# Attention stage of a hybrid layer: one group of small matmuls per block instead of two

## The chip, the cores and the metric

The kernel runs on one core of a Trainium2 chip. The metric is device microseconds of one execution. An execution that was profiled has a time of its own, and its trace spans nearly all of that time. The engines are TensorE (PE, its weight loads apart as PEld), VectorE (DVE), ScalarE (ACT), GpSimd (POOL) and SyncE (SP), each with a program of its own that it works through in order; semaphores tie them together.

## The reference, cut to what matters

One layer: an input projection, then dilated window attention beside an RWKV-7 recurrence, an output projection, and a mixture of experts. The change concerns the attention. It has 12 heads of width 64 in three groups with windows and dilations (128, 1), (512, 4) and (2048, 16); within a group each block of 128 queries sees its own 128 keys and, where there is one, the block before.

```python
p = h @ w_in
q, k, v, p_rwkv, p_gate = jnp.split(p, [...], axis=-1)
q = rms_norm(heads(q), q_norm_gain[:, None, :])
k = rms_norm(heads(k), k_norm_gain[:, None, :])
...
# per group: blocks of W queries against 2 W keys
s = jnp.einsum('bdhnqe,bdhnke->bdhnqk', qb, kb).astype(jnp.float32) * (E ** -0.5) + bias
s = jnp.where(valid, s, NEG_INF)
lse = jax.nn.logsumexp(s, axis=-1)
p = jnp.exp(s - lse[..., None])
o = jnp.einsum('bdhnqk,bdhnke->bdhnqe', p.astype(v.dtype), vb)
...
# the three groups are weighted by softmax over their lse, then projected
wts = jax.nn.softmax(jnp.stack(lses, axis=0), axis=0)
att = jnp.einsum('gbsh,gbshe->bshe', wts, jnp.stack(outs, axis=0))
mixed = gates[..., :D] * y_att + gates[..., D:] * y_rwkv
```

The sequence is 1024 long, the model 1024 wide.

## The kernel before

**Stages.** After a first stage (norm, the input projection's RWKV part, the recurrence) comes the attention stage, here from about 548 us on; at its end the output projections follow (from L1089), then the mixture of experts, which loads the weights of 32 experts. The scheduler that orders instructions by itself has been closed before the attention stage: there every engine runs in the order in which the code is written.

**Fillers.** The input projection is made of matmuls with 128x512 operands (L306, `pa<-...`, called F here), three per product, because each 32-bit factor is split in two halves. They are not run by themselves: they stand in generators in the list `fillers`, and `fill(n)` issues the next n of them. So the 1007 F of the attention stage lie between its small matmuls: 144 to a unit (the q, k and v of the next one) and, in the last unit, the columns of the gates (`rest`). An F of the gates ends, each 24, in an evacuation: VectorE L381, ScalarE L382, a store.

**Units and blocks.** There are six units (three groups, two pairs of heads), each of eight blocks. The loop at L1044 to L1070 does for each block: `fill(FA)`, 9 F; `ptrans` (L984), the transposes of the probabilities (L989, called T) and their copy to SBUF by ScalarE (L991); `scores` of the next block (L969, matmuls L976, called S; bias by VectorE L977, row maximum L979, exponentials by ScalarE L981); `fill(FU)`, 9 F; `values` (L993, matmuls L1002, called V), whose sums ScalarE copies to `Og` each fourth block (L1009). With two blocks of keys T and V are four products, with one they are two; the trace counts V, S and the two-column matmuls below twice, as two passes each.

**What else stands in the loop.** In block 1 `finish` closes the unit before: transposes of the row maxima and sums (L1019), copies by ScalarE, stores of `Og` (L1027) and `dML` (L1029) on SyncE's queue. For the last unit `finish` stands behind the loop; the later weights stand behind its stores on SyncE's queue, and `MLc`, which is loaded back from `dML` (L1109), is what the weighting of the groups begins with. In blocks 3, 4 and 5 one step each of the `prelude` of the next unit is made. Its second step are the sums of squares of q and k: 16 matmuls with two columns (L940), with two F behind every second one; VectorE makes inverse roots of them (L251 and on), GpSimd spreads those (L950), and the third step transposes these (L958) and makes the keys.

Of the kernel before, what the change touches and what calls it, by code (L numbers as in the profile page):

```python
# [23 lines left out]
NH = 8  # L24
C = 64
DEC = math.exp(-0.5)
FT, FS, FP, FA, FU, GL = 20, 6, 2, 9, 9, 10
FI, FQ, TP, FR, SQ, SG, SB, UJ, QW, QL, QT, QJ = 14, 2, 1, 16, 1, 0, 1, 1, 1, 0, 0, 1
LP, LB, LR, PF, MP, QB, GB, NY = 0, 0, 0, 1, 0, 1, 2, 2
DILS = (1, 4, 16)  # L30
# [151 lines left out]
def block_kernel(ctx, tc, I, out, dbg=None):  # L182
# [36 lines left out]
    def cc(name, i=None):  # L219
        lo, hi = CV[name]  # L220
        return cv[:, lo:hi] if i is None else cv[:, lo + i:lo + i + 1]
# [58 lines left out]
    def pb(shape):  # L280
        return psB.tile([128] + shape, F32, name="pb")
# [73 lines left out]
    for h in range(2):  # L355
        pt = psB.tile([128, 4, 128], F32, name="pb")
        for j in range(4):
            i = 4 * h + j
# [6 lines left out]
    def tstep(n=1):  # L365
        for _ in range(n):
            if side and next(side[0], 1) == 1:
                side.pop(0)
# [21 lines left out]
    def fill(n):  # L390
        while n > 0 and fillers:
            try:
                next(fillers[0])
                n -= 1
                filled[0] += 1
                if filled[0] % FI == 0:
                    tstep()
            except StopIteration:
                fillers.pop(0)
# [3 lines left out]
    def need(key):  # L403
        while key not in done:
            fill(1)
# [476 lines left out]
    def perm(ap, dil, h=None):  # L882
        L = S // dil
        v = ap.rearrange("q (r l) -> q l r", r=dil)
        return v if h is None else v[:, h * L // 2:(h + 1) * L // 2, :]
# [28 lines left out]
    def prelude(u):  # L914
        g, hp = u.g, u.hp
        nat = lambda ap: ap.rearrange("q (l r) -> q l r", r=u.dil)
        u.qT, kr, vT = qkv.pop((g, hp))
        u.bias = p4.tile([128, 2, 256], F32, name="bias")
        nb = 128 if g == 2 else 256
        for hh in range(2):  # L920
            nc.sync.dma_start(u.bias[:, hh, 256 - nb:], dBias[g, 2 * hp + hh][:, 256 - nb:])
        if g == 2:
            nc.gpsimd.memset(u.bias[64:128, :, 128:192], NEG)
        sqs = []
        for n, src in enumerate((u.qT, kr)):
            sq = p4.tile([128, S], F32, name="sq")
            nc.scalar.activation(sq, src, AF.Square)
            sqs.append(sq)
        u.Vt = p4.tile([128, 8, 128], F32, name="Vt")
        for h in range(2):  # L930
            pt = pb([4, 128])
            for j in range(4):
                i = 4 * h + j
                nc.tensor.transpose(pt[:, j], vT[:, 128 * i:128 * i + 128], ident)
            nc.scalar.activation(u.Vt[:, 4 * h:4 * h + 4], pt, AF.Copy)
        yield
        pn = pb([2, 8, 2])
        for n in range(2):
            for j in range(8):
                nc.tensor.matmul(pn[:, n, j], sqs[n][:, 128 * j:128 * j + 128], cc("ind2"), start=True, stop=True)  # L940
                if j % 2 == 1:
                    fill(2)
        u.rn = p4.tile([128, 2, 8, 2], F32, name="rqk")
        rsqrt(u.rn.rearrange("q a b c -> q (a b c)"), pn.rearrange("q a b c -> q (a b c)"), (1.0 / 64, 1e-6), None,
              [128, 32])
        nc.vector.tensor_scalar(u.rn[:, 0], u.rn[:, 0], 0.125, None, op0=ALU.mult)
        rnbs = []
        for h in range(2):
            rnb = p4.tile([128, 8, 64], F32, name="rkb")
            nc.gpsimd.tensor_tensor(rnb, u.rn[:, 1, 4 * h:4 * h + 4].rearrange("q a b -> q (a b)")[:, :, None]  # L950
                                    .to_broadcast([128, 8, 64]), one_t[:, :, None].to_broadcast([128, 8, 64]), op=ALU.mult)
            rnbs.append(rnb)
        yield
        u.kT = p4.tile([128, S], F32, name="kT")
        for h in range(2):
            pt = pb([4, 128])
            for j in range(4):
                nc.tensor.transpose(pt[:, j], rnbs[h][:, 2 * j:2 * j + 2, :].rearrange("q a b -> q (a b)"), ident)  # L958
            nc.vector.scalar_tensor_tensor(perm(u.kT, u.dil, h), nat(kr[:, h * 512:(h + 1) * 512]), gqk[:, g:g + 1],
                                           nat(pt.rearrange("q a b -> q (a b)")), op0=ALU.mult, op1=ALU.mult)  # L960
        u.Og = p4.tile([128, S], F32, name="Og")
        u.ML = p4.tile([128, 8, 4], F32, name="ML")
        nc.gpsimd.memset(u.ML[:, :, 2:4], 0.0)

    def keys(u, i):
        prev = (u.g == 0 and i > 0) or (u.g == 1 and i % 2 == 1)
        return (256, 128 * i - 128) if prev else (128, 128 * i)

    def scores(u, i):  # L969
        nk, ko = keys(u, i)  # L970
        Sb = p4.tile([128, 2, 256], F32, name="Sb", bufs=3)
        u.Sb = Sb
        for hh in range(2):
            hr = hrs[hh]
            pS = pb([256])
            nc.tensor.matmul(pS[:, 0:nk], u.qT[hr, 128 * i:128 * i + 128], u.kT[hr, ko:ko + nk], start=True, stop=True)  # L976
            nc.vector.scalar_tensor_tensor(Sb[:, hh, 0:nk], pS[:, 0:nk], u.rn[:, 0, i, hh:hh + 1],  # L977
                                           u.bias[:, hh, 256 - nk:], op0=ALU.mult, op1=ALU.add)
        nc.vector.tensor_reduce(u.ML[:, i, 0:2], Sb[:, :, 0:nk], axis=AX.X, op=ALU.max, negate=True)  # L979
        for hh in range(2):  # L980
            nc.scalar.activation(Sb[:, hh, 0:nk], Sb[:, hh, 0:nk], AF.Exp, bias=u.ML[:, i, hh:hh + 1],  # L981
                                 accum_out=u.ML[:, i, 2 + hh:3 + hh])

    def ptrans(u, i):  # L984
        nkb = keys(u, i)[0] // 128
        pP = pb([2, 2, 128])
        for hh in range(2):
            for kb in range(nkb):
                nc.tensor.transpose(pP[:, hh, kb], u.Sb[:, hh, 128 * kb:128 * kb + 128], ident)  # L989
        u.PT = p4.tile([128, 2, 2, 128], F32, name="PT")  # L990
        nc.scalar.activation(u.PT[:, :, 0:nkb], pP[:, :, 0:nkb], AF.Copy)  # L991

    def values(u, i):  # L993
        nk, ko = keys(u, i)
        nkb = nk // 128
        dil, L = u.dil, S // u.dil
        if i % 4 == 0:
            u.pO = pb([4, 128])
        for hh in range(2):
            for kb in range(nkb):  # L1000
                b = ko // 128 + kb
                nc.tensor.matmul(u.pO[hrs[hh], i % 4], u.Vt[:, b, 64 * hh:64 * hh + 64], u.PT[:, hh, kb],  # L1002
                                 start=(kb == 0), stop=(kb == nkb - 1))
        if i % 4 == 3:
            po_ = u.pO.rearrange("q a b -> q (a b)")
            if dil > 1:
                r0 = (i // 4) * (512 // L)
                o = u.Og.rearrange("q (l r) -> q r l", r=dil)[:, r0:r0 + 512 // L, :]
                nc.scalar.activation(o, po_.rearrange("q (r l) -> q r l", l=L), AF.Copy)  # L1009
            else:  # L1010
                nc.scalar.activation(u.Og[:, 128 * (i - 3):128 * (i + 1)], po_, AF.Copy)
# [22 lines left out]
    for g in range(3):  # L1034
        for hp in range(2):
            u = Unit()
# [7 lines left out]
    for _ in prelude(units[0]):  # L1044
        fill(24)
    scores(units[0], 0)
    for n, u in enumerate(units):
        nxt = units[n + 1] if n + 1 < len(units) else None
        for i in range(8):
            fill(FA)  # L1050
            ptrans(u, i)
            if i < 7:
                scores(u, i + 1)
            elif nxt is not None:
                scores(nxt, 0)
            if i == 1 and n > 0:
                finish(units[n - 1])
            if nxt is not None:
                if i == 3:
                    need(key(n + 1))  # L1060
                    pre = prelude(nxt)
                    if n + 2 < len(units):
                        fillers.append(qkv_steps(*key(n + 2)))
                    else:
                        fillers += rest
                if 3 <= i < 6:
                    next(pre, None)
            fill(FU)
            values(u, i)
    finish(units[-1])  # L1070
    s3.close()

# [627 lines left out]
```

## Time and profile before

| | us |
|---|---|
| Median of three runs | 1754.18 |
| Lowest and highest | 1747.92, 1766.67 |
| The profiled execution | 1749.15 |
| Its span in the trace | 1747.4 |
| TensorE busy | 1667.3 (95%) |
| VectorE busy | 1204.8 (69%) |
| ScalarE busy | 871.5 (50%) |
| GpSimd busy | 299.8 (17%) |

The shares are means over stages of different kinds. The page's 40 slices, of 44 us each, show the attention stage as the 13th to the 22nd: TensorE at nine tenths or more in all but the last of them, VectorE at three to six tenths, DMA at one tenth for most of it. TensorE's granted clock is a row of tenths of full speed there, and a column (PEclk) in the view by windows: 1.00 is 2.4 GHz, 0.50 is 1.2 GHz. In the view by time a row is one instruction or several of one kind in a row (x8), with its start, its busy time, and in brackets the idle time of its engine before it with what ended that. Matmuls overlap, so busy times of neighbours exceed the distance of their starts; costs are read from starts.

### The profile page before, as it was taken

What the parts mean: (1) busy time and instruction counts of PE and PEld (TensorE: products, weight loads), DVE (VectorE), ACT (ScalarE), POOL (GpSimd) and SP (SyncE); (2) the same over time, 40 slices, a digit from 0 to 9 for tenths busy, and PEclk for the clock granted to TensorE, in tenths of its full rate; (3) what the DMA queues carried; (4) which work ended last, traced back from release to release, by engine and by line L of the source; (5) the groups of instructions that cost most, each with busy time, mean ns of one, the idle gap of its engine ahead of it and who ended that gap; (6) DMA issues with size and microseconds to landing.
All of it is one profiled execution on the core that took longest, in us unless ns stands there. A gap on an engine that the chain in (4) does not pass through costs nothing. (4 is left out here: it accounts for less than half of the span.)

```text
span 1747.4 us, 25870 instructions
## 1 busy us (share of the span) xinstructions
PE 1667.3 (95%) x9395; PEld 1321.3 (76%) x9396; DVE 1204.8 (69%) x2181; ACT 871.5 (50%) x1315; POOL 299.8 (17%) x321
## 2 busy tenths in 40 slices
PE   8999999999999999999998899979999999999996
PEld 6677777777777777777777677758888888888884
DVE  5647798575664444344436666589999999998985
ACT  4523434332231233343344122278888888887774
POOL 0110113123432000000000131112222221221211
PEclk9998999799999999999999899979999999999998
DMA  8323333355762111111138884479999999999993
GB/s 292 138 74 125 95 107 115 110 193 180 232 205 85 37 38 42 43 50 43 52 113 272 253 291 144 182 250 372 375 380 373 371 368 368 371 364 372 360 371 114
DMA packets 145619, 363.44 MB, mean 208 GB/s; under 512 B 17316, under 2 KB 62772, under 8 KB 145484
## 3 DMA queue, kind: packets, MB, share of 16 engines
q1 hardware_dynamic: 123108, 303.67, 48.1%
q0 software_dynamic: 15872, 50.35, 10.3%
q10 hardware_dynamic: 6504, 7.69, 1.6%
q8 instruction: 76, 1.25, 0.3%
q14 instruction: 59, 0.48, 0.1%
HBM read 307.49 MB, written 62.29 MB: 212 GB/s over the span
## 5 line engine op out<-in xcount | busy, mean ns | idle before, releaser
L1529 PE MATMUL pb<-u,xTh 128*128 128x512 f32 x1024 | 338.6, 406 | 0.5 <-ACT xTh L1524 0.5
L306 PE MATMUL pa<-xlo,wh 128*128 128x512 f32 x736 | 307.6, 418 | 0.0
L306 PE MATMUL pa<-xhi,wl 128*128 128x512 f32 x736 | 302.3, 411 | 2.2 <-DVE wl L277 2.2
L306 PE MATMUL pa<-xhi,wh 128*128 128x512 f32 x736 | 301.5, 410 | 1.5 <-DVE raw L426 1.0
L1415 DVE TENSOR_TENSOR u<-raw,u 128x1024 fp32r<-128x1024 f32 x216 | 255.0, 1219 | 18.1 <-ACT u L1414 14.6
L1414 ACT ACTIVATE u<-raw 128x1024 fp32r<-128x1024 f32 x216 | 223.7, 1056 | 31.6 <-PE pb L1529 19.7
L1529 PEld LDWEIGHTS pb<-u,xTh 128*128 128x128 f32 x1024 | 191.4, 189 | 40.5 <-ACT xTh L1524 1.4
L1529 PE MATMUL pb<-u,xTl 128*128 128x512 f32 x512 | 207.7, 406 | 0.3 <-DVE xTl L1525 0.3
L306 PEld LDWEIGHTS pa<-xlo,wh 128*128 128x128 f32 x736 | 141.2, 192 | 40.7 <-issue 11.0
L306 PEld LDWEIGHTS pa<-xhi,wl 128*128 128x128 f32 x736 | 141.6, 192 | 34.4 <-issue 3.3
L306 PEld LDWEIGHTS pa<-xhi,wh 128*128 128x128 f32 x736 | 141.4, 192 | 34.4 <-issue 2.9
L1415 DVE TENSOR_TENSOR u<-mix,u 128x1024 fp32r<-128x1024 f32 x128 | 151.5, 1218 | 11.2 <-ACT u L1414 9.1
L1529 PE MATMUL pa<-u,hTh 128*128 128x512 f32 x512 | 143.4, 401 | 0.9 <-ACT hTh L1524 0.9
L1414 ACT ACTIVATE u<-mix 128x1024 fp32r<-128x1024 f32 x128 | 133.2, 1057 | 16.6 <-PE pb L1529 9.2
L977 DVE SCALAR_TENSOR_TENSOR Sb<-pb,rqk,bias 128x128 f32<-128x128 f32 (+1 forms) x96 | 35.5, 407 | 124.5 <-PE pb L976 116.6
L1508 POOL DMA_INDIRECT out<-row,tba x30 | 78.5, 2617 | 202.5 <-ACT u L1414 171.9
L1529 PEld LDWEIGHTS pb<-u,xTl 128*128 128x128 f32 x512 | 96.9, 189 | 18.5 <-DVE xTl L1525 1.0
L1529 PEld LDWEIGHTS pa<-u,hTh 128*128 128x128 f32 x512 | 93.5, 188 | 22.4 <-ACT hTh L1524 1.5
L275 ACT ACTIVATE wh<-wr 128x1024 fp32r<-128x1024 f32 x49 | 51.8, 1056 | 113.5 <-PE pa L306 95.1
L1529 PE MATMUL pa<-u,hTl 128*128 128x512 f32 x256 | 80.7, 396 | 1.2 <-DVE hTl L1525 1.2
L1502 POOL DMA_INDIRECT xin<-dH,tbl x32 | 38.5, 1203 | 250.7 <-PE pb L1523 247.5
L981 ACT ACTIVATE Sb<-Sb,ML 128x128 f32<-128x128 f32 (+1 forms) x96 | 42.3, 442 | 54.7 <-DVE ML L979 54.7
(415 smaller groups left out, 2872.8 us busy)
## 6 DMA issues: line engine op xcount, KB each, us to landing
raw<-in_w_expert_up SPq DMA_DIRECT2D x72, 512.0 KB, 11.7
raw<-in_w_expert_gate SPq DMA_DIRECT2D x71, 512.0 KB, 4.9
raw<-in_w_expert_down SPq DMA_DIRECT2D x71, 512.0 KB, 11.8
wr<-in_w_in SPq DMA_DIRECT2D x49, 512.0 KB, 3.5
mix<-in_w_expert_down SPq DMA_DIRECT2D x46, 512.0 KB, 13.5
mix<-in_w_expert_gate SPq DMA_DIRECT2D x42, 512.0 KB, 5.0
mix<-in_w_expert_up SPq DMA_DIRECT2D x40, 512.0 KB, 11.8
dGA<-gs POOLq DMA_DIRECT2D x32, 256.0 KB, 3.3
```

What stands on the lines that cost most here:

```text
L275: nc.scalar.activation(wh, wr, AF.Copy)
L306: nc.tensor.matmul(ps, a[:, k, :], b[:, k, hs], start=(n == 0), stop=(n == 23))
L977: nc.vector.scalar_tensor_tensor(Sb[:, hh, 0:nk], pS[:, 0:nk], u.rn[:, 0, i, hh:hh + 1], u.bias[:, hh, 256 - nk:], op0=ALU.mult, op1=ALU.add)
L981: nc.scalar.activation(Sb[:, hh, 0:nk], Sb[:, hh, 0:nk], AF.Exp, bias=u.ML[:, i, hh:hh + 1], accum_out=u.ML[:, i, 2 + hh:3 + hh])
L1414: nc.scalar.activation(hi, raw, AF.Copy)
L1415: nc.vector.tensor_tensor(lo, raw, hi.bitcast(F32), op=ALU.subtract)
L1502: nc.gpsimd.indirect_dma_start(out=dst, out_offset=None, in_=src, in_offset=bass.IndirectOffsetOnAxis(ap=idx, axis=0), bounds_check=S - 1, ...
L1508: nc.gpsimd.indirect_dma_start(out=out, out_offset=bass.IndirectOffsetOnAxis(ap=idx, axis=0), in_=src, in_offset=None, compute_op=ALU.add)
L1529: nc.tensor.matmul(ps, x, w, start=first, stop=last)
```

## The change

The matmuls of a block are put in one group: `values` moves from the end of its block to the front of the next block's group, ahead of its `ptrans`; `fill(FU)` goes, and `fill(FA)` issues 20 F instead of 9. The last block's `values` stands behind the loop, with its own `fill(FA)` ahead. In the prelude the F between the matmuls of L940 go. Lines behind L940 move up by 2 up to the loop, so that V is L1000, T L987, S L974, and the last unit's L1019 is L1017; L1089 becomes L1091.

```diff
-FT, FS, FP, FA, FU, GL = 20, 6, 2, 9, 9, 10
+FT, FS, FP, FA, GL = 20, 6, 2, 20, 10
@@ prelude
                 nc.tensor.matmul(pn[:, n, j], sqs[n][:, 128 * j:128 * j + 128], cc("ind2"), start=True, stop=True)
-                if j % 2 == 1:
-                    fill(2)
@@ the loop over units and blocks
     scores(units[0], 0)
+    last = None
     for n, u in enumerate(units):
         nxt = units[n + 1] if n + 1 < len(units) else None
         for i in range(8):
             fill(FA)
+            if last is not None:
+                values(*last)
+            last = u, i
             ptrans(u, i)
...
                 if 3 <= i < 6:
                     next(pre, None)
-            fill(FU)
-            values(u, i)
+    fill(FA)
+    values(*last)
     finish(units[-1])
```

*One block.* TensorE's program in the second block of the first unit, before: T and S as one group, nine F, V as another (`pa` and `pb` are PSUM tiles, `Sb` the probabilities, `PT` their transposes, `Vt` the values).

```order
L306 MATMUL pa<-xlo,wh 128x512
L989 MATMUL pb<-ident,Sb 128x128 x4
L976 MATMUL pb<-kT,qT 128x256 x2
L306 MATMUL pa<-xhi,wl 128x512
...
L306 MATMUL pa<-xlo,wh 128x512
L1002 MATMUL pb<-PT,Vt 64x128 x4
L306 MATMUL pa<-xhi,wl 128x512
```

The same block after the change, with 20 F to the next group; V is that of the block before, which has one block of keys:

```order
L306 MATMUL pa<-xhi,wh 128x512
L306 MATMUL pa<-xlo,wh 128x512
L1000 MATMUL pb<-PT,Vt 64x128 x2
L987 MATMUL pb<-ident,Sb 128x128 x4
L974 MATMUL pb<-kT,qT 128x256 x2
L306 MATMUL pa<-xhi,wl 128x512
```

V stands directly ahead of T. This happens 43 times; in the blocks of `i == 3` of four units F stay between V and T, since `need` runs out the queue of fillers there. The runs of F between the first L934 and the first L1089 become 60 instead of 145.

*The prelude's second step.* TensorE's program in the block with `i == 4` of the first unit, before: the two-column matmuls in pairs with two F behind each pair, eight times (`sq` the squares, `cv` a constant with two columns).

```order
L306 MATMUL pa<-xhi,wl 128x512
L989 MATMUL pb<-ident,Sb 128x128 x4
L976 MATMUL pb<-kT,qT 128x256 x2
L940 MATMUL pb<-cv,sq 128x2 x2
L306 MATMUL pa<-xhi,wh 128x512
L306 MATMUL pa<-xlo,wh 128x512
L940 MATMUL pb<-cv,sq 128x2 x2
L306 MATMUL pa<-xhi,wl 128x512
```

After:

```order
L306 MATMUL pa<-xlo,wh 128x512
L1000 MATMUL pb<-PT,Vt 64x128 x4
L987 MATMUL pb<-ident,Sb 128x128 x4
L974 MATMUL pb<-kT,qT 128x256 x2
L940 MATMUL pb<-cv,sq 128x2 x16
L306 MATMUL pa<-xhi,wl 128x512
```

All sixteen stand behind V, T and S in one group. The same happens in five units; the first unit's prelude stands ahead of the loop and has the run of L940 by itself. On VectorE the readers at this place stood so before (`rsq_u` are the means of squares, `Sb` the scores, `ML` the row maxima):

```order
L977 SCALAR_TENSOR_TENSOR Sb<-pb,rqk,bias 128x256 x2
L979 TENSOR_REDUCE ML<-Sb 128x2
L902 TENSOR_TENSOR qT<-pa,rstdB 128x128x4
L251 TENSOR_SCALAR rsq_u<-pb 128x32
L255 TENSOR_SCALAR rqk<-rsq_u 128x32
L256 TENSOR_SCALAR rqk<-rqk 128x32
```

and after:

```order
L975 SCALAR_TENSOR_TENSOR Sb<-pb,rqk,bias 128x256 x2
L251 TENSOR_SCALAR rsq_u<-pb 128x32
L977 TENSOR_REDUCE ML<-Sb 128x2
L255 TENSOR_SCALAR rqk<-rsq_u 128x32
L902 TENSOR_TENSOR qT<-pa,rstdB 128x128x4
L256 TENSOR_SCALAR rqk<-rqk 128x32
```

The first reading of the sums of squares moved ahead of the row maximum of the scores.

*The end of the stage.* TensorE's program from the last V to the output projection, before, with 47 F between L1019 and L1089:

```order
L306 MATMUL pa<-xhi,wh 128x512
L1002 MATMUL pb<-PT,Vt 64x128 x2
L1019 MATMUL pb<-ident,ML 4x128 x8
L306 MATMUL pa<-xlo,wh 128x512
...
L306 MATMUL pa<-xhi,wl 128x512
L1089 MATMUL pa<-ohi,wrh 128x512
```

After, with 28 F there:

```order
L306 MATMUL pa<-xlo,wh 128x512
L1000 MATMUL pb<-PT,Vt 64x128 x2
L1017 MATMUL pb<-ident,ML 4x128 x8
L306 MATMUL pa<-xhi,wl 128x512
...
L306 MATMUL pa<-xhi,wl 128x512
L1091 MATMUL pa<-ohi,wrh 128x512
```

The last V and `finish` moved back by 19 F. On SyncE only the store of `Og` (L1027) and one load of `raw` move a row; GpSimd's order is unchanged, and from L1089 on the orders of TensorE, ScalarE and VectorE are too.

## Rows read from the trace of the kernel before

**Rows 1.** Windows: us, busy of PE, PEld, DVE, ACT, POOL, PEclk, DMA, GB/s.

```profile
568.20:915.30 347.10, 346.04 (x1902) 255.63 (x1900) 142.11 (x301) 127.14 (x312) 18.95 (x27) 1.00 0.15 52
```

**Rows 2.** Timeline of TensorE, one block: start, busy us, engine, line, operands, count.

```profile
703.28 0.66 PE L1002 MATMUL pb<-PT,Vt 128*64 128x128 f32 x8
703.88 0.50 PE L306 MATMUL pa<-xlo,wh 128*128 128x512 f32 x1
704.22 0.40 PE L306 MATMUL pa<-xhi,wl 128*128 128x512 f32 x1
...
705.86 0.40 PE L306 MATMUL pa<-xhi,wh 128*128 128x512 f32 x1
706.09 0.60 PE L989 MATMUL pb<-ident,Sb 128*128 128x128 f32 x4
706.62 0.49 PE L976 MATMUL pb<-kT,qT 64*128 64x128 f32 x4
707.04 0.50 PE L306 MATMUL pa<-xlo,wh 128*128 128x512 f32 x1
```

**Rows 3.** Timeline of TensorE, the last values and the transposes behind them.

```profile
914.97 0.44 PE L1002 MATMUL pb<-PT,Vt 128*64 128x128 f32 x4
915.34 1.04 PE L1019 MATMUL pb<-ident,ML 128*4 128x128 f32 x8
916.14 0.48 PE L306 MATMUL pa<-xlo,wh 128*128 128x512 f32 x1
```

**Rows 4.** Timeline of TensorE, one of eight groups of L940 in a prelude.

```profile
680.88 0.50 PE L940 MATMUL pb<-cv,sq 128*128 128x2 f32 x4
681.24 0.48 PE L306 MATMUL pa<-xhi,wl 128*128 128x512 f32 x1
681.56 0.40 PE L306 MATMUL pa<-xhi,wh 128*128 128x512 f32 x1
```

**Rows 5.** Windows elsewhere in the kernel (columns as in Rows 1).

```profile
112.80:116.30 3.50, 1.76 (x8) 1.09 (x6) 0.85 (x2) 0.98 (x3) 0.00 (x0) 1.00 0.00 0
116.40:119.70 3.30, 3.04 (x14) 1.95 (x15) 2.38 (x6) 2.27 (x3) 0.00 (x0) 0.99 0.16 46
119.70:123.10 3.40, 3.40 (x10) 2.66 (x9) 3.33 (x9) 1.67 (x3) 1.03 (x2) 0.50 0.43 148
...
932.00:938.90 6.90, 6.18 (x16) 4.80 (x16) 3.97 (x10) 2.15 (x5) 0.54 (x1) 0.51 0.87 274
```

**Rows 6.** Timeline of TensorE around 119.70.

```profile
118.44 1.05 PE L578 MATMUL pb<-cv,ta 128*128 128x2 f32 x8
119.35 0.51 PE L306 MATMUL pa<-xhi,wh 128*128 128x512 f32 x1
119.67 0.62 PE L306 MATMUL pa<-xlo,wh 128*128 128x512 f32 x1
120.09 0.63 PE L306 MATMUL pa<-xhi,wh 128*128 128x512 f32 x1
```

**Rows 7.** Timeline of ScalarE, its queue and TensorE at the stage's end.

```profile
922.58 0.63 ACT L382 ACTIVATE gs<-gs 128x512 f32<-128x512 f32 x1 [3.85 <-DVE gs L381]
922.67 0.34 ACTq L1109 DMA_DIRECT2D MLc<-dML  x1
...
930.62 0.63 ACT L1080 ACTIVATE wrh<-wr 128x512 fp32r<-128x512 f32 x1 [3.61 <-DMA MLc<-dML]
931.30 0.50 PE L1089 MATMUL pa<-ohi,wrh 128*128 128x512 f32 x1 [3.92 <-ACT wrh L1080]
```

**Rows 8.** Timelines of VectorE, ScalarE and GpSimd in a prelude of 679 to 692.

```profile
679.96 0.88 DVE L977 SCALAR_TENSOR_TENSOR Sb<-pb,rqk,bias 128x256 f32<-128x256 f32 x2 [4.24 <-PE pb L976]
...
682.10 0.50 ACT L981 ACTIVATE Sb<-Sb,ML 128x256 f32<-128x256 f32 x1
...
686.90 0.19 DVE L251 TENSOR_SCALAR rsq_u<-pb 128x32 f32<-128x32 f32 x1 [2.92 <-PE pb L940]
...
689.77 2.04 POOL L950 TENSOR_TENSOR rkb<-rqk,one_t 128x512 f32<-128x512 f32 x2 [26.29 <-DVE rqk L264]
```

## The prediction, made before the changed kernel ran

> **What bounds the kernel now.** I read the page first (share of each engine and the slices), then TensorE's clock by windows, then TensorE's timeline in three places: one block of the attention loop, the groups of L940, and the end of the stage. Only the attention stage is touched. In its undisturbed part, from 568.20 to 915.30, TensorE works 346.04 of 347.10 us at granted clock 1.00, VectorE 142 us and ScalarE 127 us [rows 1]. So here the length of TensorE's program is the time, and a wait on the way counts only if it lasts longer than the fillers F (L306, 128x512) that stand before it. I call V the values (L1002), T the transposes (L989), S the scores (L976).
>
> The pitch of F is 0.234 us: seven from 704.22 to 705.86 [rows 2]. A V of eight passes takes 0.60 until the next F starts, and that F, the first behind V, takes 0.34 until its successor instead of 0.234: 0.11 is a price of leaving V. T pays nothing for being entered from F (705.86 to 706.09 is one pitch); it takes 0.53 for four and S 0.42.
>
> **The change part by part.** *F.* The number of F is the same, 1007 from the first L934 to the first L1089, so no work is added or removed; what changes is how they are cut: 145 runs before, 60 after.
>
> *V directly ahead of T.* In 43 places of the new order V is followed by T instead of F. The 0.11 behind V goes, but T may pay for the same switch. The one place where transposes follow V now is at the end: eight L1019 take 0.80 (915.34 to 916.14), 0.10 each, while T behind F takes 0.53 for four, 0.13 each [rows 2, 3]. That lies between: nothing saved and all of 0.11 saved (43 x 0.11 = 4.7). I take the middle, 0.05 each: **-2.2 us**. Both ends are kept.
>
> *L940 in one run.* Before, the sums of squares of one prelude are eight groups of four passes with two F behind each; one group takes 0.36 until the next F starts, and that F 0.32, so 0.36 + 0.09 = 0.45, or 0.11 a pass [rows 4]. L578, which has the same form (128x128 weights, two columns), stands as eight passes in one run, and the next F begins 0.91 behind its start (118.44 to 119.35), 0.11 a pass as well [rows 6]. A run of 32 passes is therefore 3.6 us, the same as eight groups: the passes, and not the switch, are the price. **0 us**; two bounds: nothing, and the 0.09 behind each of 7 groups, 6 preludes, 3.8 us.
>
> *TensorE's clock.* This is the part that I cannot read from this stage. Today every group of small matmuls has F on both sides and the clock is 1.00 throughout [rows 1]. After, five times 0.6 + 0.5 + 0.4 + 3.6 = 5.1 us (V, T, S and L940), and once 3.6 us, pass without a single 512-column matmul. What the clock does in such a stretch shows at 116.4: there TensorE works 3.04 of 3.30 us, the second part of it on eight L578 of two columns, and at 119.70 the granted clock goes from 1.00 to 0.50, that is to 1.2 GHz, and stays for 3.40 us [rows 5, 6]. The stretch ahead of it, 112.80 to 116.30, in which it works only 1.76 of 3.50 us but on F alone in its first half, was followed by no fall. So idle time is not what these rows have in common with a fall; small matmuls are. The merged run is longer and thinner than the one at 116.4. I take that each of the six runs brings one fall. The price: F's pitch is 0.42 at the lower level (119.67 to 120.09), so of a stretch at 1.2 GHz 0.19 of 0.42, 45%, is lost. Stretches last 3.40 us and, behind an idle gap, 6.90 us [rows 5]: 1.5 and 3.1, mean 2.3. **6 x 2.3 = +13.9 us.** Bounds: 0 (the clock holds) and, where each low stretch is 6.90 and half of a run of 5.1 us is stretched too (2.5 us of it lost at 0.45, 1.1), 6 x 4.2 = +25.
>
> The Trainium skill, TensorE: Matmul & The Clock Gate, section "HAM oscillation", puts the fall on gaps in which TensorE idles. By that rule the merged run, which has no idle time, keeps the clock, and the sum lacks the 13.9. The fall at 119.70 behind 3.04 busy of 3.30 us speaks against it here, and Part 1 of the same page, which lets the clock follow how busy the array has been, leaves both open.
>
> *Waits at the merged run.* VectorE's reading of the sums (L251) now stands ahead of the row maximum of the next scores, which so waits for the 3.6 us. Cover: T of these scores stands 20 F and a V behind the run, 4.7 + 0.6 = 5.3 us; from the scores' VectorE work to the end of the exponentials it is 679.96 to 682.60, 2.6 us [rows 8]. Hidden; without cover it would be those 2.6 us, four or five times. From L251 to the end of the key norms on GpSimd (686.90 to 691.81, 4.9 us [rows 8]) the cover until L958 is 20 F, V, T and S: 4.7 + 1.5 = 6.2 us. Hidden, with 1.3 us to spare. V itself gets 20 F of time for the copy of its weights instead of 9. SyncE's and GpSimd's orders stay but for one store that moves a row. 0 us.
>
> *The end of the stage.* Here a filler is worth its full time. Behind the last L1019 (915.34) stand 47 F today, and TensorE still idles 3.92 us before L1089 at 931.30. It waits for ScalarE's L1080, that for the load of MLc [rows 3, 7], and that, by the code, for the store of dML, which is made from the L1019. After, 28 F stand there: 19 F move ahead of L1019, and everything from L1019 on, the loads of the later weights on SyncE's queue included, comes 19 x 0.234 = **+4.4 us** later. What the 19 F bought behind it was only cover of that wait; TensorE's idle time grows from 3.9 to about 8. One thing comes back: the issue of MLc stands on ScalarE behind an evacuation (L382) that waited 3.85 us for the 23rd F; after, it is the 4th. Between 0 and those 3.85 us [rows 7]; since dML has to be stored first, which the evacuation does not hold up, I take a sixth, **-0.6**.
>
> *Sum.* The profiled execution has 1749.15 us (span 1747.4), under the median of 1754.18, within the runs shown. 1749.15 - 2.2 + 0 + 13.9 + 4.4 - 0.6 = **1764.7**.
>
> **The rivals.** *The clock holds* (not slower): the merged run stays at 2.4 GHz. For it: 347 us with V, T, S and L940 groups in them and no fall [rows 1], and the idle stretch at 112.80 that passed [rows 5]. Against it: 119.70 [rows 6]. Then 1749.15 - 2.2 + 4.4 - 0.6 = **1750.8**. The skill's rule of idle gaps above gives this case.
>
> *The low clock lasts* (slower): each fall costs 6.90 us and catches half of its run: 1750.8 + 25 = **1776**. For it: the run alone is as long as a stretch, so F alone may have to lift the clock. Against it: F follows at once, as at 119.70, where 3.40 were enough.
>
> *The switch is what V costs* (faster): if T's weights load beside V's passes, the whole fixed part of a V group goes, not only 0.11. That part: a V of four passes takes 0.37 until the next row [rows 3], one of eight 0.60, so a pass is 0.06 and eight are 0.46; of 0.60 + 0.11 that leaves 0.25. 43 x 0.25 = 10.8, and with the clock held 1749.15 - 10.8 + 4.4 - 0.6 = **1742**. It decides from 3.8 / 43 = 0.09 us a group on. Against it: transposes behind V take 0.10 each [rows 3], no less than others.
>
> **How the numbers follow.** Forecast 0.60 (1757 to 1771, by the two lengths of a low stretch and 5 or 6 falls), clock holds 0.20, low clock lasts 0.15, switch 0.05. The predicted time is the first's, 1764.7. The range reaches over the second and the third, 1749 to 1776, with the 4.7 of the cheaper switch at the lower end; the 1742 is left out. One per cent, 17.5 us, is about what a measurement of this kernel can tell from no change, and counts from 1749.15 to 1766.6. Above lies all but a little of the third case and about three tenths of the first: slower 0.32. Under 1731.7 not even the switch reaches by itself: faster 0.03. Same 0.65.
>
> **What would show it.** Windows over the stage: the clock at 0.50 for 3 to 7 us behind each run of L940, six times; if it is 1.00 there, the 13.9 is wrong. F behind S keeps 0.34 and T behind V about 0.5 for four; less shows the switch. L1017 later than 915.34 by 4.4 less 2.2 plus what the clock cost, and about 8 us of idle TensorE ahead of L1091; an idle time like before's would show that the 19 F were not lost. A wait of T for ScalarE of more than 0.3 us behind L940 would show that the cover failed.

## The result, and the profile after

The changed kernel takes 1764.41 us (median of 20 runs), the kernel before 1758.7 us in runs beside it: a ratio of 1.0068, with a 95% interval of 1.0047 to 1.009. It is slower by 8 to 16 us. The profiled execution of the changed kernel has 1760.64 us, with a span of 1758.9, 11.5 more than before. The page says little of why: TensorE is busy for 9.6 us more with the same instructions.

```profile
PE 1676.9 (95%) x9395; PEld 1331.0 (76%) x9396; DVE 1202.1 (68%) x2181; ACT 872.2 (50%) x1315; POOL 298.5 (17%) x321
```

The same instructions at a higher busy time point to a slower engine, and the windows show where. The first row is the attention stage up to the last V, to be set beside [rows 1]; the six behind it are all the low stretches in it; the last one lies at its end, where TensorE first idles and then starts the output projection (columns as in Rows 1).

```profile
570.60:931.20 360.60, 360.57 (x1916) 270.33 (x1914) 142.12 (x301) 127.37 (x313) 18.56 (x28) 0.96 0.16 53
580.80:584.20 3.40, 3.40 (x10) 2.67 (x10) 2.49 (x14) 0.00 (x0) 0.58 (x1) 0.52 0.00 0
628.50:635.40 6.90, 6.90 (x25) 5.93 (x25) 3.15 (x13) 1.10 (x4) 0.00 (x0) 0.52 0.00 0
690.00:693.40 3.40, 3.40 (x10) 2.67 (x9) 2.99 (x13) 0.99 (x4) 0.03 (x1) 0.53 0.00 0
744.60:748.00 3.40, 3.40 (x13) 2.82 (x13) 1.51 (x4) 1.10 (x4) 0.00 (x0) 0.53 0.00 0
799.20:806.00 6.80, 6.80 (x23) 5.82 (x23) 3.32 (x13) 1.10 (x4) 0.00 (x0) 0.52 0.00 0
853.80:860.70 6.90, 6.90 (x28) 6.22 (x28) 2.01 (x9) 1.36 (x5) 0.00 (x0) 0.52 0.01 2
942.60:952.80 10.20, 6.30 (x14) 4.53 (x15) 5.41 (x13) 2.59 (x5) 0.54 (x1) 0.51 0.91 294
```

TensorE waits for nothing in the stage (360.57 of 360.60 us) and still loses time: six falls to 1.2 GHz, 30.8 us in all, where there was none. Its timeline at the third of them:

```profile
683.16 0.39 PE L306 MATMUL pa<-xlo,wh 128*128 128x512 f32 x1
683.48 0.66 PE L1000 MATMUL pb<-PT,Vt 128*64 128x128 f32 x8
684.08 0.66 PE L987 MATMUL pb<-ident,Sb 128*128 128x128 f32 x4
684.66 0.70 PE L974 MATMUL pb<-kT,qT 64*128 64x256 f32 x4
685.30 3.73 PE L940 MATMUL pb<-cv,sq 128*128 128x2 f32 x32
688.89 0.47 PE L306 MATMUL pa<-xhi,wl 128*128 128x512 f32 x1
...
689.91 0.40 PE L306 MATMUL pa<-xhi,wh 128*128 128x512 f32 x1
690.14 0.58 PE L306 MATMUL pa<-xlo,wh 128*128 128x512 f32 x1
690.52 0.63 PE L306 MATMUL pa<-xhi,wl 128*128 128x512 f32 x1
690.95 0.63 PE L306 MATMUL pa<-xhi,wh 128*128 128x512 f32 x1
```

From 683.48 to 688.89, 5.4 us, no F runs. Then F runs at its pitch of 0.23 for a microsecond, at about 690.2 the clock falls, and F takes 0.43. In four of the six places the fall comes sooner, while L940 still runs, in three of these 1.8 us or more before its end. The fifth is one of the three: the end of the run is slower at the low clock, so that 4.47 us pass to the next F instead of 3.59.

```profile
796.77 4.61 PE L940 MATMUL pb<-cv,sq 128*128 128x2 f32 x32
801.24 0.77 PE L306 MATMUL pa<-xhi,wl 128*128 128x512 f32 x1
```

At the end of the stage the rows that answer to [rows 7] (TensorE, ScalarE and its queue):

```profile
931.59 1.03 PE L1017 MATMUL pb<-ident,ML 128*4 128x128 f32 x8
...
934.91 2.94 ACT L1082 ACTIVATE ohi<-raw 128x1024 fp32r<-128x1024 f32 x3
937.72 0.34 ACTq L1111 DMA_DIRECT2D MLc<-dML  x1
...
938.09 7.59 ACTq L1111 DMA_DIRECT2D MLc<-dML  x7
945.73 0.63 ACT L1082 ACTIVATE wrh<-wr 128x512 fp32r<-128x512 f32 x1 [6.93 <-DMA MLc<-dML]
946.41 0.80 PE L1091 MATMUL pa<-ohi,wrh 128*128 128x512 f32 x1 [7.24 <-ACT wrh L1082]
```

TensorE's idle time there is 7.24 us, where it was 3.92. Cut into four stretches, the two profiled executions compare so:

| Stretch | before | after | difference | forecast |
|---|---|---|---|---|
| Start to the first L934 (code unchanged) | 568.4 | 570.6 | +2.2 | 0 |
| First L934 to the last finish matmul | 347.7 | 361.7 | +14.0 | +16.1 |
| To the first matmul of the output projection | 15.2 | 14.1 | -1.1 | -0.6 |
| To the end | 816.1 | 812.5 | -3.6 | 0 |

The first and last stretch are not read as the change's: in the thirteen profiles of this study the first, whose code is the same in all, lasts from 561.8 to 576.1 us, and the last from 811.6 to 818.6.

### The profile page after: what moved, and what is told of

Same layout as the page of the kernel before. It is cut to its first block, busy times and chain, and to the rows that moved or that the text cites. A ratio compares the mean times of both kernels' runs of the same rounds, so it can differ in the third digit from the quotient of the medians.

```text
span 1758.9 us, 25873 instructions
## 1 busy us (share of the span) xinstructions
PE 1676.9 (95%) x9395; PEld 1331.0 (76%) x9396; DVE 1202.1 (68%) x2181; ACT 872.2 (50%) x1315; POOL 298.5 (17%) x321
## 3 DMA queue, kind: packets, MB, share of 16 engines
q0 software_dynamic: 15872, 50.35, 10.2%
## 5 line engine op out<-in xcount | busy, mean ns | idle before, releaser
L306 PE MATMUL pa<-xhi,wl 128*128 128x512 f32 x736 | 306.5, 417 | 2.3 <-DVE wl L277 2.3
L306 PE MATMUL pa<-xhi,wh 128*128 128x512 f32 x736 | 306.2, 416 | 1.5 <-DVE raw L426 1.0
L989 ACT ACTIVATE PT<-pb 128x256 f32<-128x256 f32 (+1 forms) x48 | 23.4, 488 | 106.4 <-PE pb L987 106.4
```

Of the source, the lines that this page charges most:

```text
L306: nc.tensor.matmul(ps, a[:, k, :], b[:, k, hs], start=(n == 0), stop=(n == 23))
```

## The experiments

The theory was that of the prediction: the merged run of L940 lowers the clock, the F moved ahead of finish are lost, and V ahead of T saves a little. Against it stood: the falls come from V, T and S lying together; any long stretch without F does it; the F at the end cost nothing. "The stage" is from the first L934 to the last matmul of finish, 347.7 us before and 361.7 after. The view by windows gives stage and clock of each kernel.

**Values alone.** The changed kernel, with F back in the prelude and 47 F behind the last finish.

```diff
-FT, FS, FP, FA, GL = 20, 6, 2, 20, 10
+FT, FS, FP, FA, GL = 20, 6, 2, 18, 10
...
+                if j % 2 == 1:
+                    fill(2)
...
-            fill(FA)
+            fill(FA if nxt is not None else 17)
...
-    fill(FA)
+    fill(17)
     values(*last)
```

> One part of the change alone: V directly ahead of T, one group per block; the pairs of L940 keep their F, and 47 F stand behind the last finish as before (18 F a block, 17 in the last unit). Theory (the clock falls in the merged run of L940): granted clock 1.00 from the first L934 to the last finish; that stretch takes 347.7 us before and 361.7 after; here 347.7 - 4.3 = 343.4 (0.10 us for each of 43 places, as the stretch of the changed kernel leaves it: 347.7 + 4.4 + 13.9 - 4.3 = 361.7). Ratio to before 0.9975. Rival (the clock falls because V, T and S lie together, in whatever block): low clock in this stretch here too, six falls or more, 355 us and a ratio of 1.004 or above. Second rival (grouping saves nothing and the 4.3 us came from elsewhere): 347 to 348 us.

Measured: ratio 0.9945 (0.9911 to 0.9978), the stage 343.5 us, at full clock throughout:

```profile
567.00:910.50 343.50, 343.47 (x1909) 255.61 (x1908) 143.12 (x301) 127.62 (x313) 18.95 (x27) 1.00 0.16 55
```

V, T and S together lower nothing; both rivals fall. This part of the change is a gain of 4.2 us in the stage.

**Sums alone.** The kernel before, without the F between the matmuls of L940.

```diff
-FT, FS, FP, FA, FU, GL = 20, 6, 2, 9, 9, 10
+FT, FS, FP, FA, FU, GL = 20, 6, 2, 10, 10, 10
...
-                if j % 2 == 1:
-                    fill(2)
...
-            fill(FA)
+            fill(FA if nxt is not None else FA - 1)
             ptrans(u, i)
```

> The other part alone: in the kernel before, only the F between the matmuls of L940 are taken out (10 F where 9 stood, 46 F behind the last finish); V stays by itself. Ahead of the run stand T and S, not V. Theory (a run of 3.6 us is enough for a fall): low clock behind 4 to 6 of the six runs, first L934 to last finish 347.7 + 6 to 14 = 354 to 362 us, ratio 1.003 to 1.008. Rival (only the longer group, 5.1 us with V in front, makes it fall): at most one fall, 347 to 350 us, ratio 0.999 to 1.001.

Measured: ratio 1.004 (1.0004 to 1.0076), the stage 352.1 us, with four falls of 3.4 us each, behind four of the five runs that have T and S in front; the first run, which stands alone, brought none.

```profile
561.80:913.90 352.10, 352.07 (x1910) 260.35 (x1909) 140.77 (x301) 128.23 (x313) 18.02 (x27) 0.98 0.15 52
```

The falls come with this part alone. The count was within the forecast; the stage is 2 us under it. Four falls cost 13.6 x 0.45 = 6.1, so 354.0 was due with the one F that moved. One microsecond of the gap is a wait that went (below); the rest was not traced, and fewer changes between F and L940 may be part of it.

**Two halves.** The run cut in two of 16 passes, each followed by 8 F; else as the values alone.

```diff
             for j in range(8):
                 nc.tensor.matmul(pn[:, n, j], ...)
-                if j % 2 == 1:
-                    fill(2)
+            fill(8)
```

> As the changed kernel, but the run of L940 is cut in two halves of 16 passes (1.8 us each) with 8 F (1.9 us) behind each; 18 F a block, 47 F behind the last finish. Theory (the length of the run decides): 0 to 2 falls; first L934 to last finish 343.4 to 348 us, ratio 0.9975 to 1.000. Rival (any run of L940 behind V, T and S makes it fall): six falls, 357 us, ratio 1.005.

Measured: ratio 1.0007 (0.997 to 1.0045), the stage 349.9 us, two falls, one of 3.4 and one of 10.2 us. The count is the theory's, the stage 2 us above its range, since one low stretch lasted longer than any in the stage till then: it began behind the first half and took in the second. Length matters, and half the run is not yet safe.

**The end undone.** The changed kernel, with 47 F behind the last finish instead of 28.

```diff
-            fill(FA)
+            fill(FA if nxt is not None else 18)
...
-    fill(FA)
+    fill(17)
     values(*last)
```

> The changed kernel with only the end of the stage undone: 18 F a block in the last unit and 17 ahead of its last V, so that 47 F stand behind the last finish as before, not 28. Theory: the last finish comes 19 x 0.234 = 4.4 us sooner than in the changed kernel (first L934 to last finish 357.3 instead of 361.7), of which 1.1 are lost again to the later issue of MLc: 3.3 us less in all, ratio to before 1.005 instead of 1.007; TensorE's idle time ahead of L1091 is back at 3 to 4 us. Rival (the F ahead of finish cost nothing, since the next phase hangs on other loads): the same time as the changed kernel, ratio 1.007.

Measured: ratio 1.0037 (0.9999 to 1.0075), the stage 355.6 us with five falls (27.3 us; the run that stands alone brought none), idle ahead of the projection 3.0 us. The stage is 6.1 us shorter than in the changed kernel: 1.5 are the missing fall (3.4 x 0.45), and 4.6 are left for the 19 F, for which 4.4 was forecast. The ratio is lower by 0.003, but the intervals overlap.

**F further behind the end.** Values alone, with 15 F a block in the last unit, so that 65 F stand behind the last finish.

```diff
-            fill(FA if nxt is not None else 17)
+            fill(FA if nxt is not None else 15)
...
-    fill(17)
+    fill(15)
     values(*last)
```

> The run with values alone (stage 343.5 us from the first L934 to the last finish, then 15.1 us to the output projection, of which TensorE idles some 4), with 15 F a block instead of 17 in the last unit, so that 65 F and not 47 stand behind the last finish. Theory (the F behind the last finish are cover of a wait, those ahead of it are paid): the stage is 18 x 0.234 = 4.2 us shorter, 339.3; the 15.1 stay within 1 us; TensorE's idle time there falls under 1 us. Ratio to before 0.992 if the measured 0.9945 of the run with values alone stands, and lower than that run's by 0.002. Rival (the chain of stores and loads waits for something that is not finish, so the wait moves): the 15.1 grow by 3 us or more and the ratio is that of the run with values alone.

Measured: ratio 0.9972 (0.9939 to 1.0006), the stage 339.2 us, finish to projection 15.3, as the theory had it. But the ratio is not the 0.992 of the theory, and not under that of the values alone; projection to end takes 818.6 us against 813.0. The gain in the stage was not seen at the end.

**The run apart.** The changed kernel, with 8 F between S and the run of L940.

```diff
-            fill(FA)
+            fill(FA if nxt is None or i != 5 else 12)
...
+                if i == 4:
+                    fill(8)
                 if 3 <= i < 6:
                     next(pre, None)
```

> The changed kernel, with 8 F between S and the run of L940 in the five preludes of the loop (12 instead of 20 F behind it): the run of 32 passes, 3.6 us, is whole, but V, T and S don't touch it. So far six of six runs with V, T and S in front brought a fall in the changed kernel, five of five (the first, which stands alone, none) with the end undone, four of five with T and S in front, none or one for the one that stands alone. Theory (it is the length of everything without an F, small matmuls in front included): fewer falls, 1 to 4 of the six; first L934 to last finish 361.7 - 2 to -8 = 354 to 360 us, ratio 1.001 to 1.005. Rival (a run of L940 of 3.6 us by itself is enough): six falls again, 361 to 362 us, ratio 1.007.

Measured: ratio 1.0032 (1.0003 to 1.0061), the stage 358.4 us, and six falls of six, five of 3.4 us and one of 6.8.

```profile
576.10:934.50 358.40, 358.37 (x1928) 267.02 (x1927) 143.38 (x301) 127.60 (x314) 18.59 (x28) 0.97 0.16 53
```

My theory of the length of everything without an F fell by its count, though its stage and ratio came true: the run of 3.6 us by itself can be enough. The rival had the count right and the stage 3 us too long. TensorE's timeline shows one run, with F on both sides:

```profile
690.91 0.39 PE L306 MATMUL pa<-xhi,wh 128*128 128x512 f32 x1
691.14 3.63 PE L940 MATMUL pb<-cv,sq 128*128 128x2 f32 x32
694.63 0.48 PE L306 MATMUL pa<-xlo,wh 128*128 128x512 f32 x1
...
695.42 0.47 PE L306 MATMUL pa<-xlo,wh 128*128 128x512 f32 x1
695.69 0.63 PE L306 MATMUL pa<-xhi,wl 128*128 128x512 f32 x1
```

What differs is the length of the low stretches, 30.8 us in the changed kernel and 23.9 here, and the rows show what goes with it. There are 21 falls behind whole runs, in this kernel, the changed one, the sums alone and the end undone. Seven begin 0.75 to 3.5 us before the first F behind their run of L940, and all seven last 6.8 us; thirteen begin behind the run and one 0.5 us before that F, and all fourteen last 3.4. With V, T and S in front, six of eleven falls (two kernels, first preludes included) are long; with F or T and S in front, one of ten.

**A wide run.** Values alone, with the scores of block 5 made nine or eighteen times over.

```diff
-            nc.tensor.matmul(pS[:, 0:nk], u.qT[...], u.kT[...], start=True, stop=True)
+            for _ in range((2304 // nk if i == 5 else 1)):
+                nc.tensor.matmul(pS[:, 0:nk], u.qT[...], u.kT[...], start=True, stop=True)
```

> The run with values alone, with the matmuls of the scores of block 5 made nine (two blocks of keys) or eighteen times over in each unit, so that 18 or 36 matmuls with 256 or 128 columns follow each other without an F: the same results, written again. A run is at least as long as that of L940, 3.6 to 7 us. Theory (L940 lowers the clock because its matmuls have two columns, so that nearly all its time goes to weights): no fall, clock 1.00 from the first L934 to the last finish, which takes 343.5 plus six runs, 365 to 385 us. Rival (any stretch of 5 us without a 512-column matmul lowers the clock): low clock behind five or six of these runs, some 14 us more.

Measured: one execution, 1788.25 us, the stage 384.7 us, no fall. The windows, and TensorE's timeline at two of the six runs, one of the four with 256 columns and one of the two with 128:

```profile
571.80:956.40 384.60, 384.57 (x2171) 293.54 (x2170) 143.75 (x301) 127.52 (x313) 18.98 (x27) 1.00 0.15 49
```

```profile
623.57 0.66 PE L1003 MATMUL pb<-PT,Vt 128*64 128x128 f32 x8
624.16 0.66 PE L990 MATMUL pb<-ident,Sb 128*128 128x128 f32 x4
624.75 7.28 PE L977 MATMUL pb<-kT,qT 64*128 64x256 f32 x36
631.96 0.61 PE L940 MATMUL pb<-cv,sq 128*128 128x2 f32 x4
632.43 0.48 PE L306 MATMUL pa<-xhi,wh 128*128 128x512 f32 x1
```

```profile
868.18 7.96 PE L977 MATMUL pb<-kT,qT 64*128 64x128 f32 x72
876.07 0.61 PE L940 MATMUL pb<-cv,sq 128*128 128x2 f32 x4
```

Around the first, 8.9 us pass without an F, more than in any other kernel of this study, and the clock holds. In the second, 72 passes take 7.89 us, 0.11 each, the pace of the two-column passes, and it holds too. So neither the lack of F, nor the number of small matmuls, nor their pace goes with a fall; the run of two-column matmuls does. The two kinds also differ in their weights (64 rows here, 128 in L940), and that was not varied.

**Late F alone.** The kernel before, with 63 F behind the last finish (8 F where 9 stand, in the last unit).

```diff
-            fill(FA)
+            fill(FA if nxt is not None else FA - 1)
             ptrans(u, i)
...
-            fill(FU)
+            fill(FU if nxt is not None else FU - 1)
             values(u, i)
```

> The kernel before with only the end changed: 8 F where 9 stand in the blocks of the last unit, so that 63 and not 47 F stand behind the last finish. Theory: first L934 to last finish 16 x 0.234 = 3.7 us less, 344.0; TensorE's idle time of 3.9 us ahead of the output projection all but gone; ratio 0.998. Rival: the idle time stays and finish to output projection grows by as much; ratio 1.000.

Measured: ratio 0.9967 (0.9933 to 1.0), the stage 343.9 us, idle ahead of the projection 1.3 us. The ratio is about the theory's, but its interval reaches to no change, and with the clock allowed for (last section) nothing is left of it.

**Three sizes of the end on one chip.** Values alone with 11, 47 and 65 F behind the last finish (21, 17 and 15 in place of 17 in its diff).

> One size changed, on the kernel with values alone: 11 F behind the last finish instead of 47 (21 F a block in the last unit). First L934 to last finish 343.5 + 36 x 0.234 = 351.9 us, clock 1.00. Theory (each F ahead of finish is paid in full, because all that follows starts from finish): finish to the first matmul of the experts stays at 230 us or falls by no more than the 1.2 us that MLc gave in the changed kernel; ratio to before higher than that of the values alone by 0.004 to 0.005 (7 to 8 us). Rival (the projections are bound by their loads, with DMA share 1.06 in their second 20 us, and by the gates, whose last F ends at the same time in all variants; what finish loses or wins is given back there): finish to the first matmul of the experts falls by 5 us or more, ratio higher by at most 0.002.

> The kernel with values alone once more, as the middle of the three sizes on one chip: 47 F behind the last finish, 343.5 us from the first L934 to the last finish, 230 us from there to the first matmul of the experts, ratio between 0.9945 and 0.998, all theories alike.

> The third size: 65 F behind the last finish, 339.2 us from the first L934 to the last finish, as measured. Theory (paid in full): the ratio is lower than with 47 by 0.002 (4 us). Rival (given back in the projections, as the 237.6 us from finish to the first matmul of the experts in the first profile of this kernel say): the same ratio as with 47, or a little higher.

Measured: 1.0014 (0.9982 to 1.0045), 0.9966 (0.9939 to 0.9993) and 1.0016 (0.999 to 1.0042); stages 351.9, 343.5 and 339.2 us as forecast, and from finish to the first matmul of the experts 230.6, 234.1 and 235.1 us. From 47 to 11 the loss is about what full pay would be (0.0048, 8.4 us, with wide intervals); from 47 to 65 nothing is won. Where the 4.3 us of 65 go one pair of profiles does not show: finish to the experts takes 1.0 us more with 65 F in these two, but 7.4 more in the two before (237.6 against 230.2), and 47 F alone gave 230.2 and 234.1. What the second and third 20 us of the projections show is how the waits move. First the windows with 65 F:

```profile
942.50:962.50 20.00, 17.29 (x75) 13.60 (x73) 9.28 (x13) 1.27 (x2) 2.31 (x1) 1.00 1.05 267
962.50:982.50 20.00, 11.62 (x39) 7.67 (x39) 11.29 (x12) 2.64 (x3) 2.40 (x2) 0.91 0.87 207
```

The same two windows with 47 F:

```profile
946.60:966.60 20.00, 15.96 (x59) 12.23 (x59) 9.09 (x13) 1.27 (x2) 2.37 (x1) 0.83 1.06 250
966.60:986.60 20.00, 16.01 (x58) 12.38 (x56) 11.30 (x15) 3.82 (x4) 2.40 (x1) 0.83 0.88 217
```

The DMA share is 1.05 and 1.06 in the first of the two. TensorE does nearly the same work in the 40 us, 114 matmuls with 65 F and 117 with 47, but is busy for 28.9 and 32.0 us, since its clock is 1.00 and 0.91 with 65 F and 0.83 in both with 47. With 65 F it waits more for `mix` (the gated sums) and for ScalarE's `raw`, and less for the weights `wrh` and `wrl`; its waits at L1093 add up to 15.1 us against 13.7. TensorE's waits around the projections with 65 F (waited for, us in total, times, longest):

```profile
PE pa L1093 <- DVE mix L1175: 8.4, 4, 3.5
...
PE pa L1093 <- ACT raw L1084: 4.5, 2, 3.0
```

And with 47 F:

```profile
PE pa L1093 <- ACT wrh L1084: 4.6, 1, 4.6
PE pa L1093 <- DVE wrl L1085: 4.4, 2, 4.0
PE pa L1093 <- DVE mix L1175: 3.6, 1, 3.6
PE pa L1093 <- ACT raw L1084: 0.6, 1, 0.6
```

## Why the prediction was right, and where it was not

**The forecast as a whole.** 1764.7 was forecast and 1764.41 measured. The exact hit is partly luck: the sum was made against 1749.15 and gave +15.5, while the ratio says +12.0 (8 to 16). The lower end of the range, with the 4.7 of the cheaper switch, comes to 1748.3 and not 1749; nothing hangs on it.

**The clock: right, in place, number and size, the last two with some luck.** Six falls, at the six runs of L940, three of 3.4 and three of 6.8 or 6.9 us: the mean of the two lengths that [rows 5] showed. The prediction had no reason for this even split, and its long stretch was one behind idle time; here the long ones are those that caught the last 1.8 us or more of the run. The same runs brought five falls of six with only the end undone, and four of six, all short, in the sums alone. At 45% the 30.8 us cost 13.9, as forecast. That 45% also holds elsewhere: taking 343.5 us for the stage of the values alone, 0.234 for each F moved ahead of the last finish, and 0.45 of the low time, the changed kernel comes to 343.5 + 4.4 + 13.9 = 361.8 (361.7 measured), the one with the end undone to 343.5 + 12.3 = 355.8 (355.6), the run apart to 343.5 + 4.4 + 10.8 = 358.7 (358.4), the halves to 343.5 + 6.1 = 349.6 (349.9), 11 F to 343.5 + 8.4 = 351.9 (351.9), 65 F to 343.5 - 4.2 = 339.3 (339.2). My reading of [rows 5, 6] was right in that small matmuls, not idle time, precede the fall, and too wide in "small": runs of 36 passes with 256 columns and of 72 with 128 brought none. The rival in which the clock holds (1750.8) was wrong. The Trainium skill, TensorE: Matmul & The Clock Gate, section "HAM oscillation", puts falls on gaps in which the array idles. The trace does not agree: the six falls came in a stage with TensorE busy for 360.57 of 360.60 us (the profile models where a matmul ends, so pauses within the run of L940 would not show).

**V ahead of T: the sign right, the switch right, the gain twice the forecast.** The stage of the values alone is 4.2 us shorter, not 2.2. Summing the distances of starts over the stage, F with its switches takes 4.1 us less (without what TensorE waited before the transposes L958), T 2.3 more: T behind V takes 0.58 for four (684.08 to 684.66) where behind F it took 0.53 [rows 2]. The net of 1.8 is the term of 2.2. What I left out is a wait that was in the trace before and is gone in the changed kernel, the values alone, the end undone and also the sums alone, where V is not moved but one F more stands ahead. In the view of TensorE's waits, of the stage before:

```profile
PE pb L958 <- ACT PT L991: 1.0, 4, 0.3
```

The L958 of the third prelude step waited for ScalarE's copy of the same block's transposes, by the releaser for a PSUM tile that the copy was still reading (argued, not tested). That was the one microsecond between 346.04 and 347.10 in [rows 1], and I counted it as no bound instead of asking whether the new order keeps it. The remaining 1.4 lies chiefly in S (0.6), L958 (0.5) and L934 (0.4) and was not traced further.

**L940 in one run costs nothing by itself: right.** 32 passes take 3.59 us (685.30 to 688.89) at the full clock, 0.11 each.

**The waits behind the run: right.** TensorE waits for nothing in the stage after.

**The end of the stage: right in the stage, too high for the whole.** 19 F ahead of finish lengthen the stage by 4.4; the sum above holds in five kernels. MLc is issued 6.1 us behind the L1017 (931.59 to 937.72) instead of 7.3, and finish to projection falls by 1.1 where I took 0.6; ScalarE's evacuation no longer holds it up, and whether its splits (L1082) or the stores of dML do was not told apart. The reading of [rows 7] was wrong in one point. The `wrh` that TensorE waits for is a copy of weights (`wr`) and needs no MLc: by the code it stands behind the eight issues of MLc in ScalarE's program, and it starts 0.05 us behind the last of them, before and after. Eight issues, with what they wait for in between, take 8.0 us after (937.72 to 945.68) and 7.9 before (922.67 to 930.57); the last five of those before are this row:

```profile
926.08 4.49 ACTq L1109 DMA_DIRECT2D MLc<-dML  x5
```

So the wait could be attacked by issuing MLc elsewhere or later; no run tried it. The step that does not hold to the end is "everything from L1019 on comes later": the gain of 4.3 us in the stage with 65 F was not seen in the ratio. That the projections behind it are bound by their loads and by the gates, whose last F stays where it was in the program, is argued and not shown. How much of the 4.4 reaches the end is open. The time of an execution follows its granted clock closely (below); cleaned of that, 19 F make no difference between the end undone and the run apart (3.1 and 3.0 us under before), 36 F between 47 and 11 make 1.8 us. But the longer idle time also lowers the clock longer: 13.7 us behind finish with 11 F, 6.8 with 47, another 3.1 us in these two profiles. So between a fifth (1.8 of 8.4) and all of the price; the intervals do not tell.

## What to carry to other kernels

Grouping is not one thing: tidying the two-column matmuls of six preludes into runs of 3.6 us cost 14 us through the clock, while putting V, T and S together gained 4. Judge such a run by where the same shape already stood in the trace and by the clock behind it, and try the parts of a change one by one: the better kernel here is half of the change, 0.9945 and 0.9966 of before in two sets of runs. Work moved behind a wait shortened the stage each time (by 3.8 us for 16 F, 4.3 for 18), but that gain has to be looked for at the end of the kernel, where it was not clear of noise here.

## What the runs showed of the hardware

The spread of executions goes with TensorE's clock. In one set of 35 runs of the kernel before the time goes from 1745.17 us at a mean granted clock of 0.975 to 1767.42 at 0.962. Taking twice the missing share of the span as time at 1.2 GHz, and 0.45 of that off each time, what is left scatters by 1 to 2.4 us (one standard deviation) in every kernel, where the times themselves scatter by 6 to 10. So cleaned, the means stand against before, on the same chip, at -5.1 and -5.6 (values alone, two sets), -2.0 (sums alone), -5.8 (halves), -3.1 (end undone), -3.0 (run apart), -0.1 (late F alone), -3.8 (11 F), -6.0 and -6.7 us (65 F, two sets), each with a standard error of 0.4 to 0.8. What this takes off includes the falls that a change itself brings. By these numbers 65 F are about 1 us better than 47, which is within the error, and not worse as their ratios say; of the 4.3 us of the stage that would leave a quarter.

A run of two-column matmuls of 3.6 us did not bring a fall each time: in the five preludes of the loop five of five with V, T and S in front in two kernels, five of five with F in front, four of five with T and S; the first prelude's run, which always has F on both sides, in two of four kernels; half runs in two of six preludes. The fall comes in some places while the run still goes on and in others up to 1.4 us after F has come back, so that there the rows at the fall itself show F alone. Why a run brought a fall in one place and none in another, and why at one time and not another, no run here shows.
